# The last mixer's convolution taps and weight low parts all on VectorE, the taps tied in three groups

## The chip, the cores and the metric

The kernel runs on one core of a Trainium2 chip. The metric is the device time of one execution in microseconds (us), as the median of several runs. A core has five engines with queues of their own: TensorE (PE in the profile, its weight loads PEld), VectorE (DVE), ScalarE (ACT), GpSimd (POOL) and SyncE (SP, which issues most of the DMAs). Each engine works through its instructions in the order of its queue, and waits on semaphores for what the others make.

## What is computed

Two blocks of two layers each on 512 tokens of 1024 channels. Each layer is a mixer and a SwiGLU, each followed by a residual and a LayerNorm. The change lies in the last mixer, `odd_mixer` of the second block. It has two halves: an attention of 8 heads of 64 whose logits get the running sum of a forget gate's logarithm, and a gated convolution of 31 taps on 512 channels. Shortened:

```python
def forgetting_attention(q, k, v, log_f):
    cum = jnp.cumsum(log_f.astype(jnp.float32), axis=1).transpose(0, 2, 1)
    ...
        logits = jnp.einsum("bqhd,bkhd->bhqk", q[:, q0:q1], k[:, :q1]) * scale
        logits = logits + cum[:, :, q0:q1, None] - cum[:, :, None, :q1]
        ...
        probs = jax.nn.softmax(logits, axis=-1)
        outs.append(jnp.einsum("bhqk,bkhd->bqhd", probs, v[:, :q1]))

def conformer_conv(p_d, dw_w, dw_b, cn_g, cn_b):
    h = p_d[..., :D_D] * jax.nn.sigmoid(p_d[..., D_D:])
    h = causal_dwconv(h, dw_w) + dw_b
    h = layer_norm(h, cn_g, cn_b)
    return jax.nn.silu(h)

def odd_mixer(x, w_in, forget_b, dw_w, dw_b, cn_g, cn_b, w_out):
    p = x @ w_in
    ...
    log_f = jax.nn.log_sigmoid((p[..., 3 * D_C:3 * D_C + H_C] + forget_b))
    y_c = forgetting_attention(q, k, v, log_f).reshape(bsz, s, D_C)
    y_d = conformer_conv(p[..., 3 * D_C + H_C:], dw_w, dw_b, cn_g, cn_b)
    return jnp.concatenate([y_c, y_d], axis=-1) @ w_out
```

## The kernel before

**Products in three parts.** TensorE multiplies rounded numbers, so each operand is split into a high part (the rounded value) and a low part (the rest), and `mm3` (L368 to L370) issues three matmuls: high by high, high by low, low by high. Weights come by SyncE's DMAs into `wraw` (two buffers); ScalarE rounds them to `whi` (L167), and another engine subtracts to get `wlo` (L168). That engine is VectorE, or GpSimd where the weight's name stands in `ONPOOL` and its number in the plan not in `OTHERWISE` (or the other way round). In the last mixer 27 units go to GpSimd: 3 of 128x528 and 24 of 128x1024.

**The mixer's stages.** Of the gated convolution's four groups j of 128 channels, groups 0 and 1 have their projections made by the step before. `gate(j)` takes ScalarE's sigmoid (L1380) and VectorE's product (`gl`, L1381). Then TensorE makes the forget gate's 8 columns with half of v (the 264-column product `od_v`, 4 banks). From the 8 columns VectorE makes their logarithm's sigmoid: `log_sigmoid` (L1470 to L1480) is a series of 17 small dependent operations of 128x32 on the tile `lf`, with one exponential on ScalarE. Meanwhile TensorE fills in the projections of groups 2 and 3. Two small matmuls (`sums`, L1486 and L1487) make running sums of the logarithms over the tokens; `add` and `spread` put them into the rows `ab` (L1491 to L1523), which TensorE transposes (L1530) and which become operands of the heads' scores. Then come the projections of q and k, two heads at a time (`pair`), the rest of v (`others`), and the heads. For each head and each block of 128 queries: three score matmuls, a minimum on VectorE (L1583), an exponential on ScalarE (L1584), a reciprocal, a scaling on ScalarE (L1580), transposes, the split of the transposed probabilities (`pth` on ScalarE, `ptl` on VectorE, L1065), the products with v, and the split of the output (`yh` on ScalarE, `yl` on VectorE, L376). In the gaps between these steps TensorE is given parts of the next projections (`fill`).

**The convolution.** Its taps need `gl` alone. Tap k of group j multiplies a shifted `gl` by a column of weights and adds it to `cv[j]`. For groups 0 to 2 that is one VectorE instruction (L1361 for the first, L1363 for the 30 others). For group 3 ScalarE multiplies into `tp` (one buffer, L1368) and GpSimd adds (L1369). All four `cv` are transposed on TensorE after the heads (L1702), and VectorE takes their statistics (L1704, the first statistic of the text). After that the mixer's output product goes on.

**What sets the order.** A scheduler puts each engine's instructions in order by their priorities and a model of the times. The code order gives the priority; a tap's number is set back by `OD["late"] + 20 * k + 4 * j`, so that taps stand wherever nothing more urgent is thought to be ready. In the order before, two or three taps stand between each two steps of the log-sigmoid.

Of the kernel before, what the change touches and what calls it, by code (L numbers as in the profile page):

```python
# [42 lines left out]
for _k, _w in (("g_q", 3), ("g_kv", 2), ("g_sub", 1), ("conv_w", 12), ("pool_s", 4), ("dw_w", 124),  # L43
# [9 lines left out]

ONPOOL = ("od_x", "od_v", "od_q", "od_k", "od_o", "uq_n", "ukv", "df_o", "mla_o")
OTHERWISE = (11, 12, 15, 20, 23, 24, 25, 73, 79, 80, 81, 82, 83, 84, 85, 86, 88, 90, 91, 100, 102, 103, 224, 226, 227)
NORM_ACT = (1, 3, 6, 7, 12, 13, 16, 24, 25, 26, 30)
# [7 lines left out]
    "rows": 9,  # L64
    "late": 4000,
}
ORDER = '1v23'
# [243 lines left out]
def kernel(ctx: ExitStack, tc: tile.TileContext, a: dict, out: bass.AP):  # L311
# [50 lines left out]
    def par(key, i, n=1):  # L362
        o = SM[key][0] + i
        return sm[:, o:o + n]
# [963 lines left out]
    def odd(xT, open_x, FIRST, names):  # L1328
        with pool("odd") as op_:
# [26 lines left out]

            def tap(j, k, pool=False):
                w, x = par("dw_w", CONV * j + k), gl[j][:, k:k + S]
                if not pool:
                    if k == 0:  # L1360
                        nc.vector.tensor_scalar(cv[j], x, w, par("dw_b", j), op0=OP.mult, op1=OP.add)  # L1361
                    else:
                        nc.vector.scalar_tensor_tensor(cv[j], x, w, cv[j], op0=OP.mult, op1=OP.add)  # L1363
                elif k == 0:
                    nc.scalar.activation(cv[j], x, AF.Identity, scale=w, bias=par("dw_b", j))
                else:
                    tp = op_.tile([P, S], F32, name="tp", tag="tp", bufs=1)
                    nc.scalar.activation(tp, x, AF.Copy, scale=w)  # L1368
                    nc.gpsimd.tensor_add(cv[j], cv[j], tp)  # L1369

            def conv(j):

                at = tc.cur_priority
                for k in range(CONV):
                    tc.cur_priority = at + OD["late"] + 20 * k + 4 * j
                    tap(j, k, j == 3)
                tc.cur_priority = at

# [88 lines left out]
            def log_sigmoid():  # L1467

                f = [lf[:, i].rearrange("p t h -> p (t h)") for i in range(5)]
                nc.vector.scalar_tensor_tensor(f[1], f[0], -1.0, f[0], op0=OP.mult, op1=OP.max)  # L1470
                nc.scalar.activation(f[1], f[1], AF.Exp, scale=-1.0)
                nc.vector.tensor_scalar(f[2], f[1], 2.0, None, op0=OP.add)
                nc.vector.reciprocal(f[2], f[2])
                nc.vector.tensor_mul(f[2], f[2], f[1])
                nc.vector.tensor_mul(f[3], f[2], f[2])
                nc.vector.tensor_scalar(f[4], f[3], 2.0 / 19, None, op0=OP.mult)
                for n in range(17, 2, -2):
                    nc.vector.scalar_tensor_tensor(f[4], f[4], 2.0 / n, f[3], op0=OP.add, op1=OP.mult)
                nc.vector.scalar_tensor_tensor(f[4], f[4], 2.0, f[2], op0=OP.add, op1=OP.mult)
                nc.vector.scalar_tensor_tensor(f[1], f[0], 0.0, f[4], op0=OP.min, op1=OP.subtract)  # L1480

            def sums():
# [6 lines left out]
                def add():  # L1489
                    c, o = [x.rearrange("p t h -> p (t h)") for x in (cum, lf[:, 0])]  # L1490
                    nc.vector.tensor_copy(c, ps[:, :32])  # L1491
                    nc.vector.tensor_copy(o, ps[:, 32:64])
                    for t in range(1, NT):
                        n = 8 * (NT - t)
                        nc.vector.tensor_add(c[:, 8 * t:], c[:, 8 * t:], o[:, :n])
                    nc.scalar.activation(cumh, cum, AF.Copy)
                    spread()

# [384 lines left out]
```

## Time and profile before

| what | value |
|---|---|
| median of 3 runs | 2293.64 us (2292.91 to 2295.57) |
| the profiled execution, its own time | 2293.11 us |
| its span, first to last instruction | 2291.3 us |
| TensorE busy | 2198.8 us (96%), 14076 instructions |
| VectorE busy | 1755.5 us (77%), 2813 |
| ScalarE busy | 1016.7 us (44%), 1700 |
| GpSimd busy | 239.2 us (10%), 195 |
| mean granted clock of TensorE | 0.984 |

The profile is of one execution, 0.5 us under the median. The busy shares are means over the whole span; the stage in question is found in the row of 40 slices (57.3 us each), and its limits in queries of single stretches, engines and lines of the trace. A number in brackets behind an instruction of a timeline is the engine's idle time before it, and what ended that. Three taps that stand in one row ("x3") show the time from the first one's start to the last one's end.

### The profile page before, as it was taken

To read this page: it belongs to the slowest core of one execution; us is meant where nothing else is said; L and a number is where in the kernel's file an instruction comes from. 1 tells how busy PE (TensorE), PEld (TensorE's weight loads), DVE (VectorE), ACT (ScalarE), POOL (GpSimd) and SP (SyncE) were. 2 spreads that over 40 slices of the span, in tenths; PEclk is the share of its full clock that TensorE was granted. 3 is DMA by queue.
4 is the path that set the end of the run, shared out by engine and by line. 5 is a ranking of instruction groups with operands and counts; after the bars stand their busy time and mean duration, and the time that the engine had idled before them with its cause. 6 is when DMAs were issued, how large, how long until landed. Compare 5 with 4: busy or idle time off the path is not lost. (4 is left out here: it accounts for less than half of the span.)

```text
span 2291.3 us, 35147 instructions
## 1 busy us (share of the span) xinstructions
PE 2198.8 (96%) x14076; PEld 1974.9 (86%) x14076; DVE 1755.5 (77%) x2813; ACT 1016.7 (44%) x1700; POOL 239.2 (10%) x195
## 2 busy tenths in 40 slices
PE   8999999999999999999999999999995789999997
PEld 8888999998987789999988899999884667999996
DVE  5767888886666788888675688888679667988886
ACT  4655443433665454443333344334334774443341
POOL 2200000001312100000000000000154521000001
PEclk9999999999999999999999999999997899999999
DMA  5213333333212133323232323332231102333331
GB/s 173 66 42 101 102 111 102 93 94 108 93 65 65 37 121 116 102 95 111 84 116 90 108 92 108 111 102 93 78 117 49 38 28 93 101 104 108 104 99 56
DMA packets 59363, 210.48 MB, mean 92 GB/s; under 512 B 6624, under 2 KB 6880, under 8 KB 59200
## 3 DMA queue, kind: packets, MB, share of 16 engines
q1 hardware_dynamic: 56304, 198.97, 27.1%
q0 software_dynamic: 2320, 8.23, 1.1%
q8 instruction: 110, 1.80, 0.3%
q10 hardware_dynamic: 576, 1.05, 0.1%
q14 instruction: 53, 0.43, 0.1%
HBM read 206.12 MB, written 2.10 MB: 91 GB/s over the span
## 5 line engine op out<-in xcount | busy, mean ns | idle before, releaser
L167 ACT ACTIVATE whi<-wraw 128x1024 fp32r<-128x1024 f32 (+2 forms) x528 | 520.8, 989 | 833.4 <-PE acc L369 513.0
L168 DVE TENSOR_TENSOR wlo<-wraw,whi 128x1024 fp32r<-128x1024 f32 (+2 forms) x475 | 537.0, 1131 | 108.2 <-ACT whi L167 107.4
L368 PE MATMUL acc<-xh,whi 128*128 128x256 f32 (+1 forms) x1712 | 527.6, 308 | 14.9 <-DVE vl L376 7.8
L369 PE MATMUL acc<-xl,whi 128*128 128x256 f32 (+1 forms) x1712 | 525.8, 307 | 3.1 <-DVE xl L478 3.1
L370 PE MATMUL acc<-xh,wlo 128*128 128x256 f32 (+1 forms) x1712 | 524.5, 306 | 3.2 <-DVE wlo L168 3.2
L368 PEld LDWEIGHTS acc<-xh,whi 128*128 128x128 f32 x1712 | 324.2, 189 | 41.4 <-DVE vl L376 8.0
L369 PEld LDWEIGHTS acc<-xl,whi 128*128 128x128 f32 x1712 | 324.7, 190 | 29.2 <-DVE xl L478 4.3
L370 PEld LDWEIGHTS acc<-xh,wlo 128*128 128x128 f32 x1712 | 324.6, 190 | 20.2 <-DVE wlo L168 4.3
L370 PE MATMUL acc<-xs,wlo 128*128 128x256 f32 x1216 | 341.3, 282 | 0.0
L369 PE MATMUL acc<-xql,whi 128*128 128x256 f32 x1216 | 341.0, 281 | 0.0
L368 PE MATMUL acc<-xs,whi 128*128 128x256 f32 x1216 | 339.0, 280 | 0.0
L369 PEld LDWEIGHTS acc<-xql,whi 128*128 128x128 f32 x1216 | 228.5, 188 | 5.5
L368 PEld LDWEIGHTS acc<-xs,whi 128*128 128x128 f32 x1216 | 229.6, 189 | 3.5
L370 PEld LDWEIGHTS acc<-xs,wlo 128*128 128x128 f32 x1216 | 228.1, 188 | 0.3
L168 POOL TENSOR_TENSOR wlo<-wraw,whi 128x1024 fp32r<-128x1024 f32 (+2 forms) x53 | 127.5, 2407 | 539.3 <-ACT whi L167 538.8
L386 POOL TENSOR_TENSOR lnr<-lnv,mhalf 128x1 f32<-128x1 f32 x32 | 23.7, 740 | 1271.2 <-DVE lnv L384 1271.1
L779 DVE TENSOR_TENSOR sums<-sums,acc 128x512 f32<-128x512 f32 x76 | 52.3, 688 | 86.7 <-PE acc L370 86.3
L368 PE MATMUL tr<-whi,hh 128*128 128x512 f32 (+1 forms) x296 | 117.8, 398 | 0.0
L369 PE MATMUL tr<-wlo,hh 128*128 128x512 f32 (+1 forms) x296 | 116.8, 395 | 0.0
L370 PE MATMUL tr<-whi,hl 128*128 128x512 f32 (+1 forms) x296 | 115.8, 391 | 0.0
L370 PE MATMUL ps<-whi,hl 128*128 128x512 f32 x288 | 113.7, 395 | 0.0
L368 PE MATMUL ps<-whi,hh 128*128 128x512 f32 x288 | 113.4, 394 | 0.0
(367 smaller groups left out, 4132.4 us busy)
## 6 DMA issues: line engine op xcount, KB each, us to landing
wraw<-in_gu_dram SPq DMA_DIRECT2D x176, 512.0 KB, 3.5
wraw<-in_dn_dram SPq DMA_DIRECT2D x88, 512.0 KB, 3.4
wraw<-in_ev_in_dram SPq DMA_DIRECT2D x16, 512.0 KB, 3.4
wraw<-in_mla_o_dram SPq DMA_DIRECT2D x8, 512.0 KB, 3.5
wraw<-in_df_q_dram SPq DMA_DIRECT2D x8, 512.0 KB, 3.4
wraw<-in_df_k_dram SPq DMA_DIRECT2D x8, 512.0 KB, 3.4
wraw<-in_df_v_dram SPq DMA_DIRECT2D x8, 512.0 KB, 3.5
wraw<-in_df_o_dram SPq DMA_DIRECT2D x8, 512.0 KB, 3.5
```

What stands on the lines that cost most here:

```text
L167: self.nc.scalar.activation(hi, raw[:, o:o + n], AF.Copy)
L168: eng.tensor_sub(lo, raw[:, o:o + n], hi.bitcast(F32))
L368: nc.tensor.matmul(ps, ah, bh, start=first, stop=False)
L369: nc.tensor.matmul(ps, ah, bl, start=False, stop=False)
L370: nc.tensor.matmul(ps, al, bh, start=False, stop=last)
L386: nc.gpsimd.tensor_tensor(r[:, :n], v[:, :n], mhalf[:, :n], op=OP.pow)
L779: nc.vector.tensor_add(g[:, 1:3], g[:, 1:3], v)
```

## The change

`ONPOOL` loses the last mixer's five weights (and `OTHERWISE` the three units that were an exception from them), so all 27 low parts move from GpSimd to VectorE. Group 3's 31 taps move from ScalarE and GpSimd to VectorE, one instruction each. GpSimd loses 57 instructions, ScalarE 31, and VectorE gains 58; TensorE and SyncE keep theirs, SyncE in the same order.

The taps are tied in three groups. Taps 0 to 7 of groups 0 and 1 are issued at the gates as before. Taps 8 to 11 of these two may be issued only after the log-sigmoid's last VectorE instruction (`BEHIND[0]`), all others only after the last one of the sums' chain (`BEHIND[1]`). Within the log-sigmoid and within `add` with `spread` the scheduler keeps VectorE's instructions in the order in which the code gives them (`manual_schedule`).

```diff
-ONPOOL = ("od_x", "od_v", "od_q", "od_k", "od_o", "uq_n", "ukv", "df_o", "mla_o")
-OTHERWISE = (11, 12, ..., 102, 103, 224, 226, 227)
+ONPOOL = ("uq_n", "ukv", "df_o", "mla_o")
+OTHERWISE = (11, 12, ..., 102, 103)
...
     "late": 4000,
+    "early": 8,
+    "mid": 12,
...
-            def tap(j, k, pool=False):
-                w, x = par("dw_w", CONV * j + k), gl[j][:, k:k + S]
-                if not pool:
+            BEHIND, PUT_OFF = [], []
+
+            def taps(j, k0, k1):
+
+                at = tc.cur_priority
+                for k in range(k0, k1):
+                    tc.cur_priority = at + OD["late"] + 20 * k + 4 * j
+                    w, x = par("dw_w", CONV * j + k), gl[j][:, k:k + S]
                     if k == 0:
                         nc.vector.tensor_scalar(cv[j], x, w, par("dw_b", j), op0=OP.mult, op1=OP.add)
                     else:
                         nc.vector.scalar_tensor_tensor(cv[j], x, w, cv[j], op0=OP.mult, op1=OP.add)
-                elif k == 0:
-                    nc.scalar.activation(cv[j], x, AF.Identity, scale=w, bias=par("dw_b", j))
+                tc.cur_priority = at
+
+            def chain():
+
+                BEHIND.append(next(i for i in reversed(nc.cur_bb.bb.instructions) if i.engine == mybir.EngineType.DVE))
+
+            def conv(j):
+
+                if not BEHIND:
+                    taps(j, 0, OD["early"])
+                elif len(BEHIND) == 1:
+                    PUT_OFF.append((j, 0))
                 else:
-                    tp = op_.tile([P, S], F32, name="tp", tag="tp", bufs=1)
-                    nc.scalar.activation(tp, x, AF.Copy, scale=w)
-                    nc.gpsimd.tensor_add(cv[j], cv[j], tp)
-
-            def conv(j):
-
-                at = tc.cur_priority
-                for k in range(CONV):
-                    tc.cur_priority = at + OD["late"] + 20 * k + 4 * j
-                    tap(j, k, j == 3)
-                tc.cur_priority = at
+                    with tc.issue_after(BEHIND[1]):
+                        taps(j, 0, CONV)
...
             def log_sigmoid():
 
-                f = [lf[:, i].rearrange("p t h -> p (t h)") for i in range(5)]
...
+                with tc.manual_schedule(engines={mybir.EngineType.DVE}):
+                    f = [lf[:, i].rearrange("p t h -> p (t h)") for i in range(5)]
...
+                chain()
+                with tc.issue_after(BEHIND[0]):
+                    for j in range(2):
+                        taps(j, OD["early"], OD["mid"])
+                        PUT_OFF.append((j, OD["mid"]))
...
-                    nc.scalar.activation(cumh, cum, AF.Copy)
-                    spread()
+                    with tc.manual_schedule(engines={mybir.EngineType.DVE}):
...
+                        nc.scalar.activation(cumh, cum, AF.Copy)
+                        spread()
+                    chain()
+                    with tc.issue_after(BEHIND[1]):
+                        for j, k in PUT_OFF:
+                            taps(j, k, CONV)
```

What this makes of the order: VectorE at the start of the log-sigmoid before. `lf` is the log-sigmoid's tile, `cv0` to `cv3` the convolutions, `vl` a low part of v.

```order
L1470 SCALAR_TENSOR_TENSOR lf_17151<-lf_17151 128x32
L376 TENSOR_TENSOR vl_17150<-ps_17163,vh_17149 128x256
L1363 SCALAR_TENSOR_TENSOR cv0_17059<-gl0_17055,sm_91,cv0_17059 128x512
L1363 SCALAR_TENSOR_TENSOR cv1_17060<-gl1_17056,sm_91,cv1_17060 128x512
L1472 TENSOR_SCALAR lf_17151<-lf_17151 128x32
L1363 SCALAR_TENSOR_TENSOR cv0_17059<-gl0_17055,sm_91,cv0_17059 128x512
L1363 SCALAR_TENSOR_TENSOR cv1_17060<-gl1_17056,sm_91,cv1_17060 128x512
L1473 RECIPROCAL lf_17151<-lf_17151 128x32
L1363 SCALAR_TENSOR_TENSOR cv0_17059<-gl0_17055,sm_91,cv0_17059 128x512
L1363 SCALAR_TENSOR_TENSOR cv1_17060<-gl1_17056,sm_91,cv1_17060 128x512
L1474 TENSOR_TENSOR lf_17151<-lf_17151 128x32
```

And after:

```order
L1479 SCALAR_TENSOR_TENSOR lf_17105<-lf_17105 128x32
L378 TENSOR_TENSOR vl_17104<-ps_17116,vh_17103 128x256
L378 TENSOR_TENSOR vl_17104<-ps_17117,vh_17103 128x256
L1370 SCALAR_TENSOR_TENSOR cv1_17060<-gl1_17056,sm_91,cv1_17060 128x512
L1481 TENSOR_SCALAR lf_17105<-lf_17105 128x32
L1370 SCALAR_TENSOR_TENSOR cv1_17060<-gl1_17056,sm_91,cv1_17060 128x512
L1482 RECIPROCAL lf_17105<-lf_17105 128x32
L1483 TENSOR_TENSOR lf_17105<-lf_17105 128x32
L170 TENSOR_TENSOR wlo_17483<-wraw_17431,whi_17482 128x1024
L1484 TENSOR_TENSOR lf_17105<-lf_17105 128x32
L1485 TENSOR_SCALAR lf_17105<-lf_17105 128x32
L1487 SCALAR_TENSOR_TENSOR lf_17105<-lf_17105 128x32 x8
```

Of the two or three taps between its steps one each stands ahead of two of them; the other steps follow each other, with one weight low part among them.

TensorE at the sums' matmuls before, which wait for the log-sigmoid's end:

```order
L369 MATMUL acc<-xl,whi 128x512
L370 MATMUL acc<-xh,wlo 128x512
L1486 MATMUL ps<-lf,cst 128x32
L1487 MATMUL ps<-lf,cst 128x32
L368 MATMUL acc<-xh,whi 128x512
```

And after:

```order
L372 MATMUL acc<-xh,wlo 128x512
L370 MATMUL acc<-xh,whi 128x512
L1500 MATMUL ps<-lf,cst 128x32
L1501 MATMUL ps<-lf,cst 128x32
L371 MATMUL acc<-xl,whi 128x512
```

Between the last 264-column matmul and these two stood 168 matmuls of 512 columns before; now it is 67.

VectorE among the heads before, from the first head's output of the second pair (`yl`), with the reductions, reciprocals and low parts (`ptl`) of the next scores:

```order
L376 TENSOR_TENSOR yl_18194<-ps_18195,yh_18193 64x512
L1065 TENSOR_TENSOR ptl0_18214<-tr_18227,pth0_18213 128x2x128
L1576 RECIPROCAL sums_18281<-sums_18281 128x1
L1583 TENSOR_REDUCE sums_18304<-ps_18299 128x1
L1576 RECIPROCAL sums_18291<-sums_18291 128x1
L1583 TENSOR_REDUCE sums_18317<-ps_18312 128x1
L1065 TENSOR_TENSOR ptl0_18214<-tr_18235,pth0_18213 128x2x128
L1065 TENSOR_TENSOR ptl1_18216<-tr_18235,pth1_18215 128x128
L1065 TENSOR_TENSOR ptl0_18214<-tr_18261,pth0_18213 128x2x128
```

And after, from the same output on:

```order
L378 TENSOR_TENSOR yl_18140<-ps_18141,yh_18139 64x512
L1602 TENSOR_REDUCE sums_18227<-ps_18222 128x1
L1067 TENSOR_TENSOR ptl0_18160<-tr_18173,pth0_18159 128x2x128
L1602 TENSOR_REDUCE sums_18237<-ps_18232 128x1
L1370 SCALAR_TENSOR_TENSOR cv3_17062<-gl3_17058,sm_91,cv3_17062 128x512
L1370 SCALAR_TENSOR_TENSOR cv2_17061<-gl2_17057,sm_91,cv2_17061 128x512
L1067 TENSOR_TENSOR ptl0_18160<-tr_18181,pth0_18159 128x2x128
L1067 TENSOR_TENSOR ptl1_18162<-tr_18181,pth1_18161 128x128
L1595 RECIPROCAL sums_18227<-sums_18227 128x1
L1602 TENSOR_REDUCE sums_18250<-ps_18245 128x1
```

No tap stood here before; now one to two stand between each few of the heads' operations. 50 of the 124 taps and 2 weight low parts stand behind the first head's output.

## Rows read from the trace of the kernel before

**Rows 1.** The page: busy tenths of each engine in 40 equal slices of the span.

```profile
PE   8999999999999999999999999999995789999997
...
DVE  5767888886666788888675688888679667988886
...
POOL 2200000001312100000000000000154521000001
```

**Rows 2.** Busy by stretch: us, PE, PEld, DVE, ACT, POOL (x), PEclk, DMA share, GB/s.

```profile
1675.22:1798.95 123.73, 90.69 (x477) 77.34 (x476) 122.77 (x148) 52.90 (x79) 64.16 (x30) 0.85 0.25 77
1675.22:1873.39 198.17, 151.88 (x796) 124.77 (x795) 163.06 (x263) 121.78 (x256) 92.93 (x50) 0.86 0.18 56
...
1822.14:1873.39 51.25, 43.59 (x243) 34.14 (x242) 31.11 (x90) 49.02 (x133) 19.64 (x14) 0.93 0.07 21
1874.56:1898.90 24.34, 24.11 (x122) 19.67 (x122) 13.78 (x24) 6.83 (x11) 7.81 (x4) 1.00 0.12 44
```

**Rows 3.** TensorE in time: start, us, instruction, [idle before <-what ended it].

```profile
1678.18 0.28 PE L368 MATMUL acc<-whi,xh 128*128 128x264 f32 x1
...
1689.91 0.39 PE L368 MATMUL acc<-xh,whi 128*128 128x512 f32 x1
1690.14 0.39 PE L369 MATMUL acc<-xl,whi 128*128 128x512 f32 x1
...
1721.53 0.79 PE L368 MATMUL acc<-xh,whi 128*128 128x512 f32 x1 [3.47 <-DVE gl L1381]
...
1755.40 0.61 PE L1486 MATMUL ps<-lf,cst 128*128 128x32 f32 x2 [19.71 <-issue]
...
1758.19 0.77 PE L368 MATMUL acc<-xh,whi 128*128 128x512 f32 x1 [1.76 <-DVE kk L1413]
...
1792.67 0.79 PE L368 MATMUL acc<-xh,whi 128*128 128x512 f32 x1 [7.82 <-DVE vl L376]
```

**Rows 4.** Busy by stretch, columns as in rows 2: most of the longest idle time.

```profile
1740.00:1760.00 20.00, 2.85 (x8) 2.42 (x9) 19.85 (x21) 9.95 (x15) 12.98 (x8) 0.50 0.25 79
```

**Rows 5.** VectorE and GpSimd in time: three taps alone, three beside GpSimd's four.

```profile
1726.80 2.07 DVE L1363 SCALAR_TENSOR_TENSOR cv<-gl,sm,cv 128x512 f32<-128x512 f32 x3
1728.78 0.18 DVE L1478 SCALAR_TENSOR_TENSOR lf<-lf 128x32 f32<-128x32 f32 x1
...
1737.86 7.30 DVE L1363 SCALAR_TENSOR_TENSOR cv<-gl,sm,cv 128x512 f32<-128x512 f32 x3
...
1737.86 2.35 POOL L168 TENSOR_TENSOR wlo<-wraw,whi 128x1024 fp32r<-128x1024 f32 x1
...
1744.58 1.71 POOL L1369 TENSOR_TENSOR cv<-cv,tp 128x512 f32<-128x512 f32 x1
```

**Rows 6.** Groups, 1600 to 2000: line, instruction xcount | busy, mean ns | idle before.

```profile
L1363 DVE SCALAR_TENSOR_TENSOR cv<-gl,sm,cv 128x512 f32<-128x512 f32 x90 | 97.4, 1116 | 0.6
L168 POOL TENSOR_TENSOR wlo<-wraw,whi 128x1024 fp32r<-128x1024 f32 (+1 forms) x27 | 66.8, 2475 | 66.6 <-ACT whi L167 66.4 <-PE acc L370 0.2
L1369 POOL TENSOR_TENSOR cv<-cv,tp 128x512 f32<-128x512 f32 x30 | 42.1, 1404 | 62.4 <-ACT tp L1368 62.4
L1368 ACT ACTIVATE tp<-gl,sm 128x512 f32<-128x512 f32 x30 | 21.8, 726 | 10.0 <-POOL cv L1369 9.8
```

**Rows 7.** Groups of VectorE, 1675.22 to 1873.39: first and last of six small ones.

```profile
L1361 DVE TENSOR_SCALAR cv<-gl,sm 128x512 f32<-128x512 f32 x3 | 3.7, 1239 | 0.1
...
L1520 DVE COPY ab<-cumh 128x64 f32<-128x64 f32 x1 | 1.3, 1318 | 0.0
```

**Rows 8.** VectorE in time: a low part alone; two small dependent operations.

```profile
1626.37 1.23 DVE L168 TENSOR_TENSOR wlo<-wraw,whi 128x1024 fp32r<-128x1024 f32 x1 [0.29 <-ACT whi L167]
1627.51 0.68 DVE L428 SCALAR_TENSOR_TENSOR res<-res,tr 128x512 f32<-128x512 f32 x1
...
1637.32 0.21 DVE L442 TENSOR_SCALAR lns<-lns 128x1 f32<-128x1 f32 x1
1637.57 1.29 DVE L454 SCALAR_TENSOR_TENSOR lny<-res,lns,lng 128x1024 f32<-128x1024 f32 x1
```

More of the change, by code (lines that the diff above doesn't have):

```diff
@@ L52 @@
 LNS = [(i, k) for s in ("", "_2") for i in range(2) for k in ("ln_mix_#" + s, "ln_ffn_#" + s)]
-ONPOOL = ("od_x", "od_v", "od_q", "od_k", "od_o", "uq_n", "ukv", "df_o", "mla_o")
-OTHERWISE = (11, 12, 15, 20, 23, 24, 25, 73, 79, 80, 81, 82, 83, 84, 85, 86, 88, 90, 91, 100, 102, 103, 224, 226, 227)
+ONPOOL = ("uq_n", "ukv", "df_o", "mla_o")
+OTHERWISE = (11, 12, 15, 20, 23, 24, 25, 73, 79, 80, 81, 82, 83, 84, 85, 86, 88, 90, 91, 100, 102, 103)
 NORM_ACT = (1, 3, 6, 7, 12, 13, 16, 24, 25, 26, 30)
@@ L1467, in log_sigmoid @@
             def log_sigmoid():
-                f = [lf[:, i].rearrange("p t h -> p (t h)") for i in range(5)]
[L1470 to L1480, printed above, removed]
+                with tc.manual_schedule(engines={mybir.EngineType.DVE}):
+                    f = [lf[:, i].rearrange("p t h -> p (t h)") for i in range(5)]
+                    nc.vector.scalar_tensor_tensor(f[1], f[0], -1.0, f[0], op0=OP.mult, op1=OP.max)
+                    nc.scalar.activation(f[1], f[1], AF.Exp, scale=-1.0)
+                    nc.vector.tensor_scalar(f[2], f[1], 2.0, None, op0=OP.add)
+                    nc.vector.reciprocal(f[2], f[2])
+                    nc.vector.tensor_mul(f[2], f[2], f[1])
+                    nc.vector.tensor_mul(f[3], f[2], f[2])
+                    nc.vector.tensor_scalar(f[4], f[3], 2.0 / 19, None, op0=OP.mult)
+                    for n in range(17, 2, -2):
+                        nc.vector.scalar_tensor_tensor(f[4], f[4], 2.0 / n, f[3], op0=OP.add, op1=OP.mult)
+                    nc.vector.scalar_tensor_tensor(f[4], f[4], 2.0, f[2], op0=OP.add, op1=OP.mult)
+                    nc.vector.scalar_tensor_tensor(f[1], f[0], 0.0, f[4], op0=OP.min, op1=OP.subtract)
+                chain()
[3 more added lines that the diff above has]
+                        PUT_OFF.append((j, OD["mid"]))
             def sums():
@@ L1490, in add @@
                     c, o = [x.rearrange("p t h -> p (t h)") for x in (cum, lf[:, 0])]
[L1491 to L1495, printed above, removed]
-                    nc.scalar.activation(cumh, cum, AF.Copy)
-                    spread()
+                    with tc.manual_schedule(engines={mybir.EngineType.DVE}):
+                        nc.vector.tensor_copy(c, ps[:, :32])
+                        nc.vector.tensor_copy(o, ps[:, 32:64])
+                        for t in range(1, NT):
+                            n = 8 * (NT - t)
+                            nc.vector.tensor_add(c[:, 8 * t:], c[:, 8 * t:], o[:, :n])
+                        nc.scalar.activation(cumh, cum, AF.Copy)
[4 more added lines that the diff above has]
+                            taps(j, k, CONV)
                 done(add)
```

## The prediction

> **What bounds the kernel now.** I read the page first, its engine totals and its 40 slices [rows 1], to find a stage that TensorE doesn't rule. TensorE is busy for 96% of the span, and its row is 9 nearly everywhere. In the 31st to 33rd it falls to 5, 7 and 8; GpSimd shows its highest digits from the 30th to the 32nd, 5, 4 and 5, and VectorE stands at 9 in the 31st. That is the last mixer, and the whole change lies in it. Outside it TensorE sets the pace: after the mixer's heads it is busy for 24.11 of 24.34 us [rows 2], so work moved there onto VectorE (13.78 of 24.34) is hidden.
>
> Next I cut the mixer into stages [rows 2]. From the first gate's multiply (1675.22) to the last plain tap (1798.95) VectorE is busy for 122.77 of 123.73 us, 99%, TensorE for 90.69. From the first head's output (1822.14) to the first convolution statistic (1873.39) ScalarE has 49.02 of 51.25 us, 96%, VectorE 31.11. Then I looked up TensorE's idle time in its order of time [rows 3]: 3.47, 19.71, 1.76 and 7.82 us. The longest ends with the two sums' matmuls at 1755.40. These wait for the log-sigmoid's last VectorE operation, which stands among taps. During that idle time the granted clock is 0.50, which is 1.2 GHz [rows 4].
>
> So VectorE's queue is the bound, and the question is why it is long. Three taps take 1.98 us from 1726.80 to 1728.78, 0.66 each. Three others, from 1737.86, take 7.30, and beside them GpSimd runs four instructions without a pause, from 1737.86 to 1746.29 [rows 5]. A tap that meets GpSimd is stretched. Over all 90 plain taps the sum is 97.4 us, mean 1.08 to 1.12 [rows 6] instead of 0.66.
>
> **The change part by part.** I make VectorE's list from the first gate to the first statistic, since the order shows both ends unchanged.
>
> Before: busy for 163.06 us [rows 2].
>
> Removed, the stretch. 97.35 − 90 × 0.66 = 38.0 us from the plain taps [rows 5, 6]. Six groups of small ones are stretched too, from the 3 first taps (3.7 us, where the order of 0.5 each is a tap's own) to a copy of 128x64 (1.3 us) [rows 7]; with the six, 15 instructions, 15.4 us in all, I expect 3.7 (3 × 0.5 + 12 × 0.18), so 11.7 less. GpSimd keeps next to nothing here after the change (all 27 low parts, 66.8 us, and 30 adds, 42.1 us, leave it [rows 6]), so I take the whole stretch as gone; the bounds are 49.7 and nothing (last rival).
>
> Added, convolution 3's taps: 30 × 0.66 + 0.5 = 20.3 us. ScalarE loses 21.8 us of multiplies [rows 6] and one first tap.
>
> Added, the low parts. One of 128x1024 takes 1.14 us from start to start on VectorE (1626.37 to 1627.51) [rows 8]. By the order 20 of the 27 fall between gate and statistic, one of them of half width: 19 × 1.14 + 0.6 = 22.3 us. Seven stand before or after, beside TensorE-bound work: nothing, within 2 us either way. If that cover were gone they cost 8. The weights' stream doesn't suffer: a low part needs 1.14 us where GpSimd's mean is 2.48 [rows 6].
>
> The list after: 163.1 − 38.0 − 11.7 + 20.3 + 22.3 = 156.0 us. That is only 7 us shorter. The rest of the gain must come from packing, which is the second part of the change: of the 198.17 us before, VectorE idles 35, nearly all after the last tap, where nothing is left for it beside the heads. After the change 50 of the 124 taps and 2 low parts stand behind the first head's output in VectorE's order. So I split the list there. Behind it: 31.1 as before [rows 2], plus 50 × 0.66 and 2 × 1.14, 66.4 us. Ahead of it: 156.0 − 66.4 = 89.6 us, of which 22 up to the log-sigmoid's end.
>
> The tied chains. Ahead of the first forget-gate entry stand 11 taps, 2 gate multiplies and 4 low parts, 12.4 us. TensorE ends that product at 1689.9, 14.7 us after the gate [rows 3], so VectorE waits up to 2.5 us. In a row, two small dependent operations start 0.25 us apart for 0.21 of work [rows 8]; some 13 gaps of 0.04 give 0.5, and ScalarE's exponential and rounding are two round trips. Between 0.5 and 5, I take 2.8, as a tap and two low parts of values still stand under the first trip. Together 5.3 us of waiting, behind which all later taps queue. In return the log-sigmoid ends near 1675.2 + 22 + 5 = 1702. TensorE has 67 matmuls of 512 columns ahead of the sums instead of 168; at 0.23 us [rows 3] it reaches them at 1689.9 + 15.6 = 1705.5. The wait of 19.71 us goes, and with it the clock's fall. What is late next is VectorE itself.
>
> TensorE's own list from the start of its 264-column product (1678.18) to the first head's output is 86.7 us (counts of the order by the durations of [rows 3]), as long as VectorE's 89.6. Two full lists wait on each other, so I don't take the 99% of before but the 95.7% that ScalarE had among the heads, for both parts: 89.6 / 0.957 = 93.6 and 66.4 / 0.957 = 69.4. Statistic at 1675.2 + 5.3 + 93.6 + 69.4 = 1843.5, against 1873.4: 29.9 us earlier. Less 2 for the collision of late taps with the heads' reductions, 28. What follows the statistic is unchanged. The profiled execution took 2293.1 us around its span of 2291.3; 2293.1 − 28 = 2265, and the median of the runs is half a us above it: **2266**.
>
> **The rivals.** First, the *half clock*. Behind the first head's output TensorE has only about 31 us of full-clock work in 69 us. If the clock stays at 1.2 GHz there, as at 0.50 in [rows 4], its list is 63 us, as long as VectorE's 66. For two such lists I take TensorE's share of that stretch before, 43.59 of 51.25, 85%: 66.4 / 0.85 = 78.1, 8.7 later: 2275. For it: the idle share. Against it: 0.93 was granted there before [rows 2].
> In the Trainium skill, "TensorE: Matmul & The Clock Gate", section "HAM oscillation — how this bites in real kernels", short bursts of matmuls between idle pauses run at half rate; no run before shows that for the heads with taps among them.
>
> Second, *taps in the heads' way*. Each score needs a VectorE reduction, and its probabilities a VectorE low part; an in-order queue puts one to four taps ahead of these. If each tap there is paid in full on top of the heads' own pace, the last part takes 51.25 + 35.3 = 86.5 instead of 69.4: 2283. If taps and heads add up like this before the first output too, the rest of the gain goes: no change, 2294. Against it: ScalarE, the heads' bound before, loses its 22 us of multiplies.
>
> Third, the slower side: *the stretch isn't GpSimd's*. Then 124 taps at the mean of 1.08 last 52 us longer than I put them, the list is 208 us, and the statistic comes some 50 us later than forecast: 2316. The point from which it decides is a mean tap of 0.66 + 28 / 124 = 0.89 us; above it the kernel is slower. Against it stands the pair of [rows 5], 1.98 and 7.30 for the same three taps.
> The Trainium skill, "Perfetto Trace Analysis", section "Optimizing Scalar/DVE Operations", says that a saturated VectorE is relieved by moving work to other engines, and that GpSimd may not help since it shares a port with VectorE. Its first half speaks against taking multiplies back from ScalarE: counted alone, that and the low parts add 42.6 us to a full queue and give 2336. The second half agrees with the 7.30 of [rows 5].
>
> And on the near side: VectorE never waits but for TensorE's 2.5 us, with the list at 152 us by start-to-start times: statistic at 1830, 2250.
>
> **How the numbers follow.** Forecast with its own range 2257 to 2273: 48 in 100. Half clock, 2273 to 2277: 20. Taps in the way, 2278 to 2284: 12, no change by it or by several of these at once: 6. Better than forecast, 2250 to 2255: 6. Slower, by the stretch that stays (4) or by a collision that no row shows (4): 8. The first three make 80: range 2255 to 2284. About 0.2%, 4.6 us, is what a measurement of this kernel can tell from no change. Faster: 48 + 20 + 12 + 6 = 86; same 6; slower 8.
>
> **What would show each step.** Right: GpSimd's digits are 0 in the 30th to 32nd slice; the taps' mean is 0.66 to 0.70 over 120; low parts there at 1.1 to 1.2; the sums' matmuls near 1706 with no wait above 3 us; the first head's output near 1774; VectorE above 93% up to the first statistic at about 1845. Half clock: granted clock under 0.7 in the last 70 us before the statistic. Taps in the way: idle ScalarE and TensorE there, released by VectorE's reductions. Wrong altogether: taps at 0.9 or more with GpSimd idle, or a first head's output after 1790.

## The result and the profile after

The changed kernel takes 2255.36 us (median of 4 runs, 2253.95 to 2257.42) against 2293.27 us of the kernel before (4 runs): 0.9834 of the time, 95% interval 0.9817 to 0.9851. That is 38 us less, where the prediction had 28. The profiled execution's span is 2253.7 us against 2291.3.

The page after, its rows of busy tenths, as [rows 1]:

```profile
PE   8999999999999999999999999999999889999997
...
DVE  5767988887666688888765588888679987988886
...
POOL 2200000001321100000010000000010000000001
```

GpSimd's 5, 4 and 5 are now 1, 0 and 0, and TensorE's 5, 7, 8 are 9, 8, 8. The mixer by stretches, columns as in [rows 2]: from the first gate to the first head's output, from there to the first statistic, and both together.

```profile
1673.58:1770.07 96.49, 96.04 (x551) 82.69 (x551) 93.83 (x173) 60.63 (x108) 0.00 (x0) 1.00 0.33 103
1770.07:1836.56 66.49, 52.26 (x250) 39.14 (x249) 64.06 (x143) 44.61 (x119) 0.00 (x0) 0.87 0.06 18
1673.58:1836.56 162.98, 148.30 (x799) 121.82 (x799) 157.89 (x315) 105.24 (x227) 0.00 (x0) 0.95 0.22 68
```

The stage took 198.17 us in [rows 2] and takes 162.98 now: 35.2 of the 37.6 us. Of the rest 1.6 lie ahead of the first gate (1673.58 instead of 1675.22) and 0.8 behind the first statistic. VectorE is busy for 157.89 us instead of 163.06, 5 us less; the big change is that its idle time falls from 35.1 to 5.1. TensorE is now full ahead of the first output, 96.04 of 96.49 us, and VectorE nearly (97%); behind it VectorE has 96%. So ahead of the first output two engines are now full at once.

The log-sigmoid's end and the sums, VectorE and TensorE in time (start, us, instruction, x count):

```profile
1696.53 1.78 DVE L1487 SCALAR_TENSOR_TENSOR lf<-lf 128x32 f32<-128x32 f32 x8
1698.35 0.19 DVE L1488 SCALAR_TENSOR_TENSOR lf<-lf 128x32 f32<-128x32 f32 x1
1698.57 0.19 DVE L1489 SCALAR_TENSOR_TENSOR lf<-lf 128x32 f32<-128x32 f32 x1
...
1709.53 2.07 DVE L1370 SCALAR_TENSOR_TENSOR cv<-gl,sm,cv 128x512 f32<-128x512 f32 x3
1711.52 0.68 DVE L1389 TENSOR_TENSOR gl<-cv,acc 128x512 f32<-128x512 f32 x1
```

```profile
1676.60 0.28 PE L370 MATMUL acc<-whi,xh 128*128 128x264 f32 x1
...
1703.64 0.40 PE L370 MATMUL acc<-xh,whi 128*128 128x512 f32 x1
1703.88 0.30 PE L1500 MATMUL ps<-lf,cst 128*128 128x32 f32 x2
```

The log-sigmoid ends at 1698.8 (1755.3 before), and TensorE reaches the sums at 1703.88 with no idle time in front of them, where [rows 3] show 19.71 us. Three taps in a row behind that take 1.99 us, 0.66 each. Over the mixer the taps are (line, count | busy, mean ns | idle before), against [rows 6]:

```profile
L1370 DVE SCALAR_TENSOR_TENSOR cv<-gl,sm,cv 128x512 f32<-128x512 f32 x120 | 85.6, 742 | 0.5
```

And the low parts from the first gate to 1849 (us, VectorE busy (x), GpSimd busy (x), clock, DMA):

```profile
1673.58:1849.00 175.42, 25.05 (x21) 0.00 (x0) 0.95 0.21 66
```

120 taps are busy for 85.6 us, 0.71 each, where 90 took 97.4. The mean of 742 ns counts each tap from its start to its own end, and the next one starts before that end. The 21 low parts take 1.19 us each.

### The profile page after: what moved, and what is told of

It is laid out like the page before. It is cut to its first block, busy times and chain, and to the rows that moved or that the text cites. A ratio compares the mean times of both kernels' runs of the same rounds, so it can differ in the third digit from the quotient of the medians.

```text
span 2253.7 us, 35104 instructions
## 1 busy us (share of the span) xinstructions
PE 2194.6 (97%) x14076; PEld 1971.3 (87%) x14076; DVE 1753.4 (78%) x2871; ACT 998.2 (44%) x1669; POOL 132.1 (6%) x138
## 5 line engine op out<-in xcount | busy, mean ns | idle before, releaser
L170 DVE TENSOR_TENSOR wlo<-wraw,whi 128x1024 fp32r<-128x1024 f32 (+2 forms) x502 | 568.2, 1133 | 126.2 <-ACT whi L169 123.3
L370 PEld LDWEIGHTS acc<-xh,whi 128*128 128x128 f32 x1712 | 322.4, 188 | 25.6 <-DVE kl L1097 0.5
L371 PE MATMUL ps<-wlo,hh 128*128 128x512 f32 x288 | 113.2, 393 | 0.0
L430 DVE SCALAR_TENSOR_TENSOR res<-res,acc 128x512 f32<-128x512 f32 x87 | 59.1, 683 | 58.1 <-PE acc L372 57.7
```

Of the source, the lines that this page charges most:

```text
L170: eng.tensor_sub(lo, raw[:, o:o + n], hi.bitcast(F32))
L370: nc.tensor.matmul(ps, ah, bh, start=first, stop=False)
L371: nc.tensor.matmul(ps, ah, bl, start=False, stop=False)
L430: nc.vector.scalar_tensor_tensor(y, y, ALPHA if first else 1.0, ps, op0=OP.mult, op1=OP.add, accum_out=SUMS[t][:, c:c + 1] if sums else None)
```

## The experiments

Each was timed beside the kernel before on the same chip; the medians of before in the four sets were 2292.4, 2292.7, 2292.6 and 2294.5 us. A difference from the changed kernel compares medians of two sets, so 2 us of it can be the chip. My theory going in: GpSimd's absence shortens VectorE's list, and the tie lets the taps fill the heads' time; the two parts add up.

### The tie alone, the move alone

E1 keeps the tie of the change and puts everything back on GpSimd and ScalarE that was there before:

```diff
-ONPOOL = ("uq_n", "ukv", "df_o", "mla_o")
+ONPOOL = ("od_x", "od_v", "od_q", "od_k", "od_o", "uq_n", "ukv", "df_o", "mla_o")
...
             def conv(j):
+                if j == 3:
+                    for k in range(CONV):
...
+                            nc.scalar.activation(tp, x, AF.Copy, scale=w)
+                            nc.gpsimd.tensor_add(cv[j], cv[j], tp)
...
+                    return
```

> The kernel before with the tie alone: GpSimd keeps its 27 low parts and convolution 3's adds, ScalarE its multiplies; the other three convolutions' taps are tied in the three groups and the two chains stand in a row. My theory is that the gain of 38 us has two parts, which add up roughly: a VectorE queue without GpSimd beside it (about 7 us of list), and an order in which taps stand among the heads instead of ahead of them. In this order 84 of the 93 plain taps stand ahead of the first head's output and 9 behind it, so the taps' stretch of 1.08 us on average stays and little moves behind: first output near 1803 instead of 1822, 2275 us (2268 to 2283), the sums' wait of 19.71 us gone. Rival A, the gain is GpSimd's absence alone: no change, 2290 or more. Rival B, the gain is the tie alone: 2260 or less.

Measured 2277.43 us, 0.9933 (0.9919 to 0.9948): 15 us faster than before. E2 keeps the move and drops the tie:

```diff
             def conv(j):
-                if not BEHIND:
-                    taps(j, 0, OD["early"])
...
+                taps(j, 0, CONV)
...
-                with tc.manual_schedule(engines={mybir.EngineType.DVE}):
...
-                with tc.issue_after(BEHIND[0]):
...
-                    with tc.issue_after(BEHIND[1]):
```

> The changed kernel without the tie: all taps and low parts on VectorE, none on GpSimd, the taps placed by their priorities alone, as before. In this order 120 of the 124 taps stand ahead of the first head's output and 65 ahead of the log-sigmoid's end, and 301 matmuls of 512 columns ahead of the sums. My theory: taps at 0.66 us, the log-sigmoid ends near 1752, first output near 1806, then the heads' own 51 us with nothing of the taps beside them: 2280 us (2272 to 2287). Rival A (GpSimd's absence alone is the gain): 2262 or less. Rival B (the tie alone): 2288 or more.

Measured 2267.49 us, 0.9886 (0.987 to 0.9903): 25 us faster. Neither rival holds, and 15 + 25 = 40 is near the 37 to 38 of both: the parts add up in size. E1 came out at my number; E2 12 us better: its first output came at 1800 instead of 1806, and the heads took 48.7 us instead of 51, which is 8 of the 12. E2 by stretches, gate to first output to first statistic:

```profile
1674.70:1800.20 125.50, 106.82 (x557) 89.34 (x557) 122.80 (x220) 61.88 (x108) 0.00 (x0) 0.89 0.25 80
1800.20:1848.90 48.70, 41.12 (x238) 31.57 (x237) 36.09 (x98) 41.14 (x119) 0.00 (x0) 1.00 0.08 23
```

VectorE's work is that of the changed kernel, 158.9 us against 157.9. Without the tie 120 of the 124 taps are done ahead of the first output, behind it VectorE is busy for 36.09 of 48.70 us only, and its idle time is 15.3 instead of 5.1 us. These 10 us are nearly all of the 12 that the tie is worth on top of the move. TensorE, in E2, waits 8.15 us for the rows of the sums, and in E1 twice:

```profile
1766.62 0.66 PE L1534 MATMUL tr<-ident,ab 128*128 128x128 f32 x2 [8.15 <-DVE ab L1525]
```

```profile
1708.86 0.39 PE L1513 MATMUL ps<-lf,cst 128*128 128x32 f32 x1 [8.42 <-issue]
...
1757.04 0.45 PE L1602 MATMUL ps<-kk,qq 128*128 128x128 f32 x1 [14.93 <-DVE kk L1434]
```

In E1 (the lower two) the tied order has the sums 47 us earlier than before, but VectorE, stretched by GpSimd, is late with everything: 8.42 us for the log-sigmoid (the profile names no releaser, but its last operation ended at 1708.76) and 14.93 for the first low part of k.

From the first gate to the first head's output, the kernel before and then E1:

```profile
1675.22:1822.14 146.92, 108.29 (x555) 90.62 (x554) 131.95 (x174) 72.76 (x124) 73.28 (x37) 0.84 0.22 68
```

```profile
1675.70:1796.50 120.80, 95.18 (x527) 80.90 (x527) 117.79 (x162) 62.12 (x111) 64.05 (x28) 0.89 0.24 74
```

That the two parts add up in size doesn't make their causes the ones I had in mind. The move alone shortens this stretch by 21 us (146.92 to 125.50), but VectorE's work in it by only 9 (131.95 to 122.80): the rest is VectorE's idle time, 15.0 us before and 2.7 in E2, and TensorE's falls from 38.6 to 18.7. The tie alone leaves only 9 taps behind the first output, so its 15 us can't come from filling the heads' time; it ends this stretch 26 us sooner, and TensorE's idle time there falls from 38.6 to 25.6. What each of these waits is worth by itself no run shows.

### Which of GpSimd's two tasks it was

E3 is the changed kernel with `ONPOOL` and `OTHERWISE` of before (first part of E1's diff), E4 the changed kernel with convolution 3 back on ScalarE and GpSimd (second part).

> The changed kernel with the 27 low parts back on GpSimd; all 124 taps on VectorE and tied. Before, 93 us of GpSimd work in the stage lengthened VectorE's by 50, 0.53 us for each; the 51 us of low parts in the stage would cost 27 and take 22 off VectorE. 91 of 124 taps stand ahead of the first head's output instead of 74. Theory: 2264 us (2258 to 2270), taps' mean 0.85 to 0.9 us ahead of the first output, 0.66 to 0.7 behind it. If the low parts are what matters, 2275 or more; if GpSimd's low parts don't stretch the taps, 2250.

Measured 2271.93 us, 0.991 (0.9895 to 0.9924), 16.6 above the changed kernel. I had counted on 9.

> The changed kernel with convolution 3 back on ScalarE and GpSimd (one multiply and one add per tap); the low parts and the other 93 taps on VectorE, tied. By the same 0.53 us per us the 42 us of adds cost 22 and take 20 off VectorE; 22 taps stay behind the first output. Theory: near the changed kernel, 2258 us (2254 to 2264), taps' mean 0.85 us. If the chain of multiply and add, which has one buffer between the engines, ends last, the transposes of convolution 3 come late and the time is 2270 or more.

Measured 2257.87 us, 0.9846 (0.9831 to 0.986), 2.5 above the changed kernel, as counted. The two groups of GpSimd, E3 first, then E4 (mean ns behind the busy time):

```profile
L170 POOL TENSOR_TENSOR wlo<-wraw,whi 128x1024 fp32r<-128x1024 f32 (+1 forms) x20 | 50.3, 2520 | 90.9 <-ACT whi L169 90.9
```

```profile
L1389 POOL TENSOR_TENSOR cv<-cv,tp 128x512 f32<-128x512 f32 x30 | 45.5, 1518 | 112.0 <-ACT tp L1388 112.0
```

The stage, gate to first statistic, in E4 (E3's follows further down):

```profile
1674.60:1838.40 163.80, 145.89 (x795) 120.28 (x793) 156.23 (x284) 122.43 (x256) 45.55 (x30) 0.95 0.22 68
```

VectorE's 156.23 us are some 19 more than the changed kernel's 157.89 less the 20.3 of convolution 3's taps; for E3 the same sum gives 40. So for about as much GpSimd time the low parts cost far more. On top of the tie the move is worth 22 us (E1 to the changed kernel); 17 to 20 of these are the low parts' (E3 to the changed kernel, E1 to E4) and 2.5 to 5.5 the taps'. Why the low parts cost more per us is the last run's question.

### GpSimd's work that nobody waits for

E5 adds GpSimd work to the changed kernel that nobody waits for. E6 has one addition and 90 fills, which read nothing, in their place; E12 has fewer and longer instructions.

```diff
                 nc.vector.tensor_mul(gl[j][:, CONV - 1:], cv[j], pa)
                 conv(j)
+                if j == 0:
+                    tp = op_.tile([P, S], F32, name="tp", tag="tp", bufs=1)
+                    for _ in range(30):
+                        nc.gpsimd.tensor_add(tp, gl[0][:, :S], gl[0][:, CONV - 1:])
```

> The changed kernel with GpSimd work that nobody waits for: from the first gate on, 30 additions of 128x512 of a convolution's input to itself shifted, into a scratch tile that nobody reads. VectorE's, ScalarE's and TensorE's instructions and their order stay. At about 1.4 us each they fill some 42 us from 1674 on. My theory is that GpSimd's work by its mere presence stretches VectorE's taps, 0.53 us for each us: 22 us more VectorE work ahead of the first head's output, of which VectorE has 3 to spare: 2274 us (2266 to 2282), the taps of the first 40 us at a mean of 1.0 or more and those after at 0.66 to 0.75. Rival, the stretch came from waits of taps for GpSimd's or ScalarE's results: 2255, no change.

Measured 2276.87 us, 0.9931 (0.9916 to 0.9946): 21.5 us slower than the changed kernel, for work that has no reader. E6:

```diff
+                    nc.gpsimd.tensor_add(tp, gl[0][:, :S], gl[0][:, CONV - 1:])
+                    for _ in range(90):
+                        nc.gpsimd.memset(tp, 0.0)
```

> As the run with 30 additions, but one addition and 90 fills of the same scratch tile with a constant, about 0.5 us each, so GpSimd is busy as long but reads nothing. If any work of GpSimd stretches the taps: 2270 to 2280, as with the additions. If only work that reads its operands from the same memory does, no change: 2255 (2252 to 2258), taps at 0.66 to 0.75. The Trainium skill, SBUF — State Buffer, in the list of practical consequences under its table of ports, says the second: a VectorE instruction with two inputs there contends with a GpSimd instruction that reads it, not with one that only writes.

Measured 2255.34 us, 0.984 (0.9823 to 0.9856): no change. GpSimd and VectorE in time, in E5:

```profile
1675.78 45.81 POOL L1394 TENSOR_TENSOR tp<-gl 128x512 f32<-128x512 f32 x30 [9.98 <-DVE gl L1389]
```

```profile
1675.74 1.41 DVE L1368 TENSOR_SCALAR cv<-gl,sm 128x512 f32<-128x512 f32 x1
...
1680.09 4.58 DVE L1370 SCALAR_TENSOR_TENSOR cv<-gl,sm,cv 128x512 f32<-128x512 f32 x3
1684.58 2.11 DVE L170 TENSOR_TENSOR wlo<-wraw,whi 128x1024 fp32r<-128x1024 f32 x1
1686.62 1.58 DVE L1370 SCALAR_TENSOR_TENSOR cv<-gl,sm,cv 128x512 f32<-128x512 f32 x1
...
1688.12 0.68 DVE L1389 TENSOR_TENSOR gl<-cv,acc 128x512 f32<-128x512 f32 x1
...
1721.79 1.41 DVE L1370 SCALAR_TENSOR_TENSOR cv<-gl,sm,cv 128x512 f32<-128x512 f32 x2
```

and in E6:

```profile
1676.44 44.07 POOL L1395 MEMSET tp<- 128x512 f32 x74
```

```profile
1677.99 2.33 DVE L1370 SCALAR_TENSOR_TENSOR cv<-gl,sm,cv 128x512 f32<-128x512 f32 x3
1680.23 1.22 DVE L170 TENSOR_TENSOR wlo<-wraw,whi 128x1024 fp32r<-128x1024 f32 x1
```

(74 of the 90 fills, up to 1720, where the view ends). A first tap in the changed kernel:

```profile
1674.38 0.55 DVE L1368 TENSOR_SCALAR cv<-gl,sm 128x512 f32<-128x512 f32 x1
```

The same three taps take 4.58 us beside additions and 2.33 beside fills (one low part stands between them and the next in both). From 1721.6 on, when the additions are done, the taps of E5 are at 0.7 again. The gate's multiply at 1688.12, whose second input is a matmul's bank, isn't stretched. This is what the Trainium skill says in SBUF — State Buffer, section "Who interferes with whom": two inputs in SBUF, the memory of these tiles, contend with a GpSimd instruction that reads it, one input doesn't outside VectorE's two-port modes, and for two inputs a GpSimd instruction that only writes doesn't matter; here 4.58, 0.68 and 2.33 us agree. A first tap (L1368) has one such input besides its scalars, and it took 1.41 us beside the additions instead of 0.55. Its form, `tensor_scalar`, is among those that the Trainium skill names in the same section as able to enter a two-port mode and then to contend; that this one ran in such a mode no row shows.

E12 replaces the 30 additions by 18 subtractions of twice the length:

```diff
+                    tp = op_.tile([P, 2, S], BF16, name="tp", tag="tp", bufs=1)
+                    two = [x[:, None, :].to_broadcast([P, 2, S]) for x in (gl[0][:, :S], gl[0][:, CONV - 1:])]
+                    for _ in range(18):
+                        nc.gpsimd.tensor_sub(tp, *two)
```

> The changed kernel with 18 idle subtractions of 128x1024 on GpSimd (a weight low part's length; operands read from a convolution's input, each half twice, into a scratch tile of 16-bit numbers that nobody reads) from the first gate on, in place of the 30 additions of 128x512. If one takes 2.4 us they fill some 43 us, as the additions did. Low parts back on GpSimd cost 16.6 us, more than the 9 I had counted. If that is because a longer GpSimd instruction costs VectorE more per us (0.8 instead of 0.51): 2288 us (2282 to 2293), VectorE's list ahead of the first output longer by 34 us. If it costs the same per us, and the low parts' extra came from the order and the waits: 2276 us (2272 to 2280), as with the additions.

Measured 2285.21 us, 0.9963 (0.9949 to 0.9977): nearer to the first number than to the second. VectorE's busy time up to the first head's output in E12, and the same row of E5:

```profile
1674.16:1799.90 125.74, 102.42 (x547) 86.58 (x546) 124.12 (x174) 60.64 (x108) 43.18 (x18) 0.89 0.26 79
```

```profile
1674.94:1792.60 117.66, 103.06 (x554) 87.42 (x554) 116.05 (x173) 60.81 (x108) 43.54 (x30) 0.91 0.27 84
```

GpSimd is busy for 43 us in both. VectorE's 93.83 us of the changed kernel become 116.05 with 30 instructions and 124.12 with 18: 22.2 and 30.3 more, 0.51 and 0.70 per us. In E12 a tap takes as long as the GpSimd instruction beside it:

```profile
1682.03 7.29 DVE L1370 SCALAR_TENSOR_TENSOR cv<-gl,sm,cv 128x512 f32<-128x512 f32 x3
1689.24 3.02 DVE L170 TENSOR_TENSOR wlo<-wraw,whi 128x1024 fp32r<-128x1024 f32 x1
1692.18 2.48 DVE L1370 SCALAR_TENSOR_TENSOR cv<-gl,sm,cv 128x512 f32<-128x512 f32 x1
```

2.4 us each, where the 18 subtractions take 44.51 / 18 = 2.5 from start to start. So the two engines go instruction by instruction: for each GpSimd instruction one VectorE instruction with two inputs in SBUF gets through. From start to start a low part takes 2.04 us beside additions (1684.58 to 1686.62) and 2.94 beside subtractions. Less the 1.14 and 0.66 us that a low part and a tap take alone, meeting an addition costs VectorE 0.84 to 0.90 us and meeting a subtraction 1.74 to 1.80, whichever of the two meets it.

As a simple estimate, a GpSimd instruction costs VectorE its own length less the VectorE instruction's: 30 x (1.45 − 0.74) = 21 and 18 x (2.40 − 0.74) = 30, with the mean lengths of the two GpSimd groups (43.5 / 30 and 43.2 / 18) and the tap's mean of 0.742. That is near both runs. For E4's 30 additions, which come one by one behind ScalarE's products, it gives 23 us where 19 were measured. It also says why a low part on GpSimd is a bad trade: 1.8 us of VectorE's time each (2.52 − 0.74) to save 1.14. In E3 it gives 20 x 1.78 = 36 us. The stage's row there:

```profile
1674.20:1854.50 180.30, 148.23 (x794) 122.56 (x792) 173.69 (x295) 103.66 (x225) 50.31 (x20) 0.91 0.20 62
```

VectorE's 173.69 us are 40 more than the changed kernel's 157.89 without 20 low parts of 1.19; the last 4 stay open.

### What bounds VectorE's part now, and whether the tie's details matter

E7 leaves out the last five taps of convolutions 2 and 3.

```diff
                 for k in range(k0, k1):
+                    if j > 1 and k > 25:
+                        continue
```

> The changed kernel without the last five taps of convolutions 2 and 3 (ten taps left out, so that part of the convolution isn't computed). In the order all ten are missing behind the first head's output, 40 stand there instead of 50; ahead of it everything stays. If VectorE bounds that part (96% busy there): 10 x 0.66 us less, 2249 us (2247 to 2251). If the heads' own chain through ScalarE and TensorE bounds it: less than 2 us, 2254 or more.

Measured 2251.18 us, 0.9817 (0.9802 to 0.9832): 4.2 us less than the changed kernel, between my two cases. Behind the first output:

```profile
1771.60:1832.50 60.90, 48.88 (x243) 36.45 (x242) 57.46 (x133) 43.04 (x117) 0.00 (x0) 0.89 0.07 20
```

VectorE's 64.06 us fall by 6.6, the stretch by 5.6, and VectorE's share from 96 to 94%. So this part follows VectorE's work nearly one to one, though the whole kernel gains only 4.2. The heads' chain is the next bound: in E2 the heads with 4 taps among them take 48.70.

E8 drops the two fixed rows and keeps the groups (`manual_schedule` gone, `issue_after` kept). E9 drops the second border, so that all later taps wait for the log-sigmoid alone. E10 sets the borders at 16 and 20 instead of 8 and 12.

> The changed kernel without the two chains' fixed rows: the three groups of taps stay tied, but the scheduler may put other VectorE work between the small operations. Theory: the tie of the groups is what moves the log-sigmoid ahead, and the row moves its end by 1 to 2 us, which TensorE's 67 matmuls ahead of the sums hide (5 us to spare): no change, 2255 (2252 to 2258). If the row carries the gain of the tie: 2262 or more.

Measured 2256.23 us, 0.984 (0.9825 to 0.9855): no change.

> The changed kernel with two groups instead of three: every tap after the eighth of convolutions 0 and 1 may be issued after the log-sigmoid's chain, none is held for the sums' chain. In the order 72 taps instead of 74 stand ahead of the first head's output, and 67 matmuls ahead of the sums as before. Theory: the tie to the log-sigmoid does it, the second tie moves small operations by a tap or two, which nobody waits for: no change, 2255 (2252 to 2258). If the second tie is needed: 2262 or more, with a wait of TensorE at the transposes of the sums' rows.

Measured 2256.31 us, 0.9842 (0.9827 to 0.9856): no change.

> The changed kernel with the groups' borders at taps 16 and 20 instead of 8 and 12. In the order 32 taps and 10 low parts instead of 16 and 7 stand ahead of the log-sigmoid's end, 132 matmuls of 512 columns instead of 67 ahead of the sums, 37 taps instead of 50 behind the first head's output. Theory: VectorE's list is the same and is full in both parts; ahead of the first output it becomes VectorE's 102 us instead of TensorE's 96, behind it 55 instead of 64: 2257 us (2254 to 2261), the sums near 1721 without a wait of 3 us. If the early sums themselves bring the gain (the heads' first scores wait for them): 2263 or more.

Measured 2254.77 us, 0.9836 (0.982 to 0.9853): no change. E10 by stretches, and TensorE at the sums:

```profile
1674.90:1781.90 107.00, 104.78 (x586) 88.75 (x585) 103.96 (x189) 63.90 (x112) 0.00 (x0) 1.00 0.31 99
1781.90:1836.30 54.40, 42.02 (x213) 31.27 (x214) 52.60 (x128) 41.51 (x115) 0.00 (x0) 0.91 0.03 11
```

```profile
1720.38 0.30 PE L1500 MATMUL ps<-lf,cst 128*128 128x32 f32 x2
```

The sums come at 1720 here, 16 us later than in the changed kernel, the first output 12 us later, and the first statistic at the same time. VectorE is 97% busy in both parts. So on top of the move the tie doesn't pay by the date of the sums, between 1704 and 1720, but by leaving enough taps behind the first output to fill the heads' time: 50, 52 or 37 of 124 do, 4 (E2) don't.

E11 gives the four first taps to ScalarE, which has a third of its time free.

```diff
-                        nc.vector.tensor_scalar(cv[j], x, w, par("dw_b", j), op0=OP.mult, op1=OP.add)
+                        nc.scalar.activation(cv[j], x, AF.Identity, scale=w, bias=par("dw_b", j))
```

> The changed kernel with the four first taps (one multiply and add of the bias each) on ScalarE instead of VectorE, one instruction each. VectorE's list gets 4 x 0.46 = 1.8 us shorter, ScalarE has a third of its time free. If VectorE bounds both parts: 2253.5 us (2252 to 2255), which the rounds can hardly tell from 2255.4. If ScalarE's part comes late (the second tap waits for it, and the queue behind that): 2256 or more.

Measured 2258.01 us, 0.9848 (0.9833 to 0.9863), its runs between 2255.1 and 2258.9: no gain, though the stage was 1.3 us shorter than the changed kernel's (161.7) in its profiled execution, the fastest of its runs. Why the others took 3 us longer stays open. No version that computes everything beats the changed kernel by more than the measurement can tell.

## Why the prediction came out as it did

The time lies 0.4 us inside the range's lower end and outside the forecast's own 2257 to 2273. The runs spread from 2253.95 to 2257.42, so that the median falls inside at all is luck. The sign, the place and the mechanism were right: GpSimd's stretch of VectorE goes, and taps fill VectorE's idle time. The gain was 10 us too small. By the steps:

- **The list.** Predicted 156.0 us of VectorE work from gate to statistic, measured 157.89. Right within 2, but two misses partly cancel in it: ahead of the first output 93.83 where I had 89.6, behind it 64.06 where I had 66.4. That GpSimd's reading instructions stretch VectorE's is shown by E5, E6 and E12, and the third rival (2316) is gone. The taps' mean is 0.71 or 0.74 us, by the way of counting, a little above the 0.66 to 0.70 that I had named as a sign.
- **The low parts.** Put at 1.14 each, 22.3 in all; the 20 there took 1.19. I took the stretch as one sum and didn't ask which of GpSimd's two tasks caused it. E3 and E4 show that moving the low parts was most of the move's gain on top of the tie.
- **The log-sigmoid and the sums.** Predicted to end near 1702 and 1705.5, measured 1698.8 and 1703.9, without a wait. That the wait of 19.71 us goes was right, but E10 shows that a date 16 us later costs nothing, and E8 that the fixed row isn't what pays either. What I called packing is most of the gain: VectorE's work fell by 5 us, its idle time by 30.
- **The share of 95.7%: this term failed.** I took 5.3 us of waits at the chains, and for two full lists ScalarE's share among the heads: 4.0 and 3.0 us. Of these 12.3 us, 5.1 were there, 2.7 ahead of the first output and 2.4 behind it: 7 us. Beside each other TensorE had 99.5% and VectorE 97% ahead of the first output, so two full lists ran side by side. My reading is that they need not wait on each other as long as neither waits for the other's latest result, and that the scheduler had put taps wherever VectorE would have waited; no run tests that. TensorE's own list was mis-sized too: I had 86.7 us, and from 1676.60 to the first output at 1770.07 it took 93.5 almost without a pause. That the first output came within 4 us of the forecast is therefore in part luck: both lists were longer and the waits shorter than I had them.
- **The 2 us for late taps** among the heads' reductions: nothing of it is seen. Behind the first output VectorE's idle time is 2.4 us in all (66.49 less 64.06), less than the 3.0 that I had given the share alone.
- **Ahead of the gate and behind the statistic**: put at nothing, 1.6 and 0.8 us gained in the profiled executions. The first gate came between 1673.1 and 1675.1 in the profiles of the kernels whose low parts are all on VectorE, though their code up to there is the same, so I don't count the 1.6 as explained.

28 − 1.9 + 7.2 + 2 + 1.6 + 0.8 = 37.7, which is the span's gain of 37.6 but for rounding. The rivals:

- **The half clock** came, and no cost of it is seen. Around an idle time of 3.38 us that ended at 1781.94 TensorE's granted clock was 0.57 for 10 us, so mostly at the lower of its levels of 1.2 and 2.4 GHz, and 0.74 for the next 10:

```profile
1781.94 0.47 PE L1588 MATMUL ps<-kb,qa 128*128 128x128 f32 x1 [3.38 <-ACT e L1603]
```

```profile
1780.00:1790.00 10.00, 7.40 (x28) 6.41 (x29) 9.56 (x20) 5.83 (x17) 0.00 (x0) 0.57 0.18 52
1790.00:1800.00 10.00, 7.77 (x30) 5.26 (x29) 9.85 (x21) 7.92 (x20) 0.00 (x0) 0.74 0.01 2
1800.00:1810.00 10.00, 8.49 (x49) 6.11 (x49) 9.94 (x26) 8.11 (x25) 0.00 (x0) 1.00 0.00 0
```

VectorE (the third of the busy times) stayed at 96 to 99%, so the slower matmuls lay beside its work, and the clock was back at 1.00 with taps still among the heads. The rival's sign was a clock under 0.7 up to the statistic; over that part it was 0.87.

- **Taps in the heads' way**: their sign is there, their price isn't. ScalarE's scalings among the heads wait 8.7 us in the changed kernel, nearly all for VectorE's reciprocals, and 0.1 in E2, which has 4 taps there (behind the first output; line, count | busy, mean ns | idle before):

```profile
L1599 ACT ACTIVATE e<-e,sums 128x384 f32<-128x384 f32 (+3 forms) x22 | 12.4, 571 | 8.7 <-DVE sums L1595 8.6
```

```profile
L1584 ACT ACTIVATE e<-e,sums 128x256 f32<-128x256 f32 (+3 forms) x22 | 12.3, 567 | 0.1
```

So the taps do hold up the heads, which take 66.49 us instead of E2's 48.70. But VectorE is busy for 96% of that, so the heads wait for its full list, and nothing is paid on top of it; the rival had the taps on top of the heads' own pace, 86.5 us. There was room for the taps since the heads' own bound before was ScalarE, which now has 44.61 of 66.49 us.

## What to carry over

Two engines that go instruction by instruction, as GpSimd and VectorE did here, make a trade per instruction, not per us. By the estimate above an off-loaded instruction costs the other engine about its own length less one of the other's, so the long instructions on the slower engine were the worst to off-load, though nobody waited for them. And when a queue is full in one stage and idle in the next, look first for work without a near reader that can be held back for the idle stage: here that was worth 12 us on top of the move, and each of the three sets of borders that I tried did as well.

## What the runs showed that I had not expected

The stretch is one to one: beside GpSimd subtractions of 2.4 us each tap took 2.4 us, beside additions, 1.5 us from start to start, 1.5. GpSimd pays less than VectorE: its addition took 1.45 us on average in E5, the single one in E6 1.09. A GpSimd instruction that only writes cost VectorE nothing (90 fills of 0.54 us; the median differs by 0.02 us from the changed kernel's). Small dependent VectorE operations in a row took 0.22 us each (eight in 1.78 us).
